# Regrouping the attention of a decoder block between dense products: four groups of small products become three

## The chip, the cores and the metric

The kernel runs on one core of a Trainium2 chip. The metric is the device time of one execution in microseconds (us), the median of several runs. The engines are called TensorE (PE in the profile; its weight loads are PEld), VectorE (DVE), ScalarE (ACT), GpSimd (POOL) and SyncE (SP, which here only issues transfers).

## The reference

One decoder layer over 256 tokens of 1024 channels, in float32. Two attention branches of 8 heads with 64 channels each run side by side; their outputs are gated and summed, and a gated feed-forward block with a short convolution follows.

```
h = rms_norm(x, attn_norm_g)
qa, ka, va, qb, kb, vb, f_logit, g_logit = split(h @ w_in)
qa, ka = partial_rope(rms_norm(heads(qa))), partial_rope(rms_norm(heads(ka)))
o_a = moba_attention(qa, ka, va)          # one block of 256 keys: causal softmax
qb, kb = rms_norm(heads(qb)), rms_norm(heads(kb))
log_f = log_sigmoid(f_logit + b_forget)
o_b = forgetting_attention(qb, kb, vb, log_f)   # scores + c[t] - c[s], c = cumsum(log_f)
gates = sigmoid(g_logit + b_gate)
merged = gates[0] * (o_a @ w_branch_moba) + gates[1] * (o_b @ w_branch_fox)
x = x + merged @ w_out
u, g = split(rms_norm(x, ffn_norm_g) @ w_ffn_up)
x = x + (silu(causal_conv(g)) * u) @ w_ffn_down
```

With 256 tokens the first branch's block selection leaves each query its own block, so both branches are causal attention over all 256 keys; the second adds a bias from the running sum c.

## The kernel before

**Dense products.** Every weight is split into a high half and a low half of fewer bits (`load`, lines 116 to 139): ScalarE copies the raw weight into `whi` (L134), VectorE subtracts to get `wlo` (L135). The activations are split in the same way, and a dense product is three products, high by high, high by low and low by high, summed in one PSUM bank. `project` (L236) does this for q, k and v of both branches (`project(0..5)`) and, through `gate` (L443), for eight half products of the gates. One half of a weight feeds 12 products of 512 columns on TensorE (L245).

**Loads.** `use` (L141) asks for a half of a weight and first calls `load` up to five halves ahead. Where `state["hold"]` is true it doesn't, and a later explicit `load(...)` catches up. While `state["behind"]` names two instructions, the split on ScalarE is ordered behind the first and that on VectorE behind the second.

**PSUM.** All products go to eight banks of 512 columns, taken in turn (`bank`, `banks`); a new use waits until the engines that read the old content are done.

**Attention.** It runs as small products put between the dense ones:

- `turn_one` (L282) turns a finished q or k with 16 transposes (L289) into two banks; two copies with a gain bring it to SBUF, on ScalarE (L297) or, where named in `vector`, on VectorE (L295).
- `forget_c` (L352) sums log_f by a product (L357), copies on VectorE (L359, L360), stores to DRAM and loads it back spread over all partitions, both issued from ScalarE's queue (L362, L363). `forget_bias` (L365) adds the mask on VectorE.
- `scores(branch, pair)` (L377) does two heads: products on TensorE into two banks (L387), four masked reductions that read the banks on VectorE (L392), four exponentials on ScalarE (L395), and a reciprocal and four scalings on VectorE (L397, L400).
- `turn(branch, pair)` (L406) turns the probabilities of two heads with 12 transposes (L414) into two banks and copies them out, two copies on ScalarE (L404) or, where named, on VectorE (L416).
- `values(branch, pairs)` (L420) multiplies two pairs' turned probabilities with v (L428) into one bank; ScalarE takes the high half (L430), VectorE the low (L431).

**Order.** TensorE runs in the order in which the code is written (`manual_schedule` names it alone). On the other engines a planner orders the instructions when the program is built, by its own estimate of when each becomes ready: of those that are ready on an engine, it takes the one written first. That order is then fixed. The stretch that matters is lines 482 to 530. There the attention's small products form four groups between dense products: in the middle of the second k's product (L487 to L495), after the first gate half product (L503 to L505), after the fourth (L512 to L517), and after the eighth (L523 to L530).

Of the kernel before, what the change touches and what calls it, by code (L numbers as in the profile page):

```python
# [30 lines left out]
RB, HB, AHEAD = 3, 6, 5  # L31
# [10 lines left out]
def decoder_block(ctx, tc, a, out):  # L42
    nc = tc.nc
# [6 lines left out]
    def T(shape, tag, bufs=1, dt=F32):  # L50
        return sb.tile(shape, dt, tag=tag, bufs=bufs, name=tag)
# [33 lines left out]
    pos = {c: i for i, c in enumerate(chunks)}  # L85
    split = {}
    state = {"next": 0, "raw": None, "ahead": AHEAD, "hold": False, "behind": None}
# [18 lines left out]
    def home(n):  # L106

        slot = (n - state["base"] - AHEAD - 1) % (HB + 3) if AHEAD < state["ahead"] else 3
        if slot > 2:
            return T([P, 1024], "whi", HB, F32R), T([P, 1024], "wlo", HB, F32R)  # L110
        if slot == 2:
            return [T([P, 1024], "qn", 3, F32R) for _ in range(2)]
        both = T([P, 2, 1024], ("V", "bias")[slot], 1, F32R)
        return both[:, 0], both[:, 1]

    def load(upto):
        while state["next"] <= min(upto, 2 * len(chunks) - 1):
            i, h = divmod(state["next"], 2)
            state["next"] += 1
            if i < 2:  # L120
                lead(2 * i + h)
                continue
            c = chunks[i]
            if h == 0:
                w = 1024 if i == 2 else 2048
                src = a[c[0]]
                for j in (c[1] - (c[0] == "qkv"), *c[2:]):
                    src = src[j]
                raw = state["raw"] = T([P, 2048], "raw", RB)
                for j in range(2048 // w):  # L130
                    nc.sync.dma_start(raw[:, j * w:(j + 1) * w], src[:, j * w:(j + 1) * w])
            raw = state["raw"][:, h * 1024:(h + 1) * 1024]
            hi, lo = home(2 * i + h)
            whi = nc.scalar.activation(hi, raw, AF.Copy)  # L134
            wlo = nc.vector.tensor_tensor(lo, raw, hi.bitcast(F32), op=ALU.subtract)  # L135
            if state["behind"]:
                after(whi, state["behind"][0])
                after(wlo, state["behind"][1])
            split[c, h] = (hi, lo, whi)
# [142 lines left out]
    def turn_one(n, br, isk, vector=()):  # L282
        dst = T([P, 4, S], f"{'qk'[isk]}T{br}")
        two = banks()
        for t in range(NT):
            for b in range(4):
                c = slice((4 * t + b) * HD, (4 * t + b + 1) * HD)
                for r, (rows, eye) in enumerate(parts):
                    nc.tensor.transpose(two[r][:, c], n[rows, t, 2 * b:2 * b + 2].rearrange("p h d -> p (h d)"), eye)  # L289
        for r in range(2):  # L290
            to = dst.rearrange("p b (t r c) -> p r t b c", t=NT, r=2)[:, r]
            src = two[r].rearrange("p (t b c) -> p t b c", t=NT, b=4)
            gain = col(C_QG + 2 * br + isk)
            if r in vector:
                last = nc.vector.tensor_scalar_mul(to, src, gain)  # L295
            else:
                first = nc.scalar.activation(to, src, AF.Copy, scale=gain)  # L297
                last = first
        turned[br, isk] = dst
        return first, last  # L300
# [51 lines left out]
    def forget_c():  # L352
        lf = fg["lf"]
        cp = bank()
        c0, c1 = (cp[:NH, t * P:(t + 1) * P] for t in range(NT))
        for t, c in enumerate((c0, c1)):
            nc.tensor.matmul(c, lf[:, t], tri, start=True, stop=True)  # L357
        cT = T([P, 2, 384], "pT", 4)[:NH, 0, 0:S]
        nc.vector.tensor_copy(cT, cp[:NH, 0:S])  # L359
        nc.vector.tensor_scalar_add(cT[:, P:S], cT[:, P:S], cT[:, P - 1:P])  # L360
        cd = dr.tile([NH, S], F32, name="cd")
        nc.scalar.dma_start(cd, cT)  # L362
        nc.scalar.dma_start(bias[:, :, P:P + S], bass.AP(tensor=cd.tensor, offset=cd.offset, ap=[[0, P], [S, NH], [1, S]]))  # L363
# [13 lines left out]
    def scores(br, pair):  # L377
        s = T([P, 2, 384], "s", 4)
        nm = T([P, 2, 2], "nm", 4)
        l = T([P, 2, 2], "l", 4)  # L380
        sps = banks()
        for t in range(NT):
            for j in range(2):
                dst = sps[j][:, t * P:t * P + (t + 1) * P]
                ts, us = slice(t * P, (t + 1) * P), slice(0, (t + 1) * P)
                rows = parts[j][0]
                nc.tensor.matmul(dst, turned[br, 0][rows, pair, ts], turned[br, 1][rows, pair, us], start=True, stop=True)  # L387
        for j in range(2):
            h = 2 * pair + j
            sp = sps[j]  # L390
            for i, c in enumerate((slice(0, 128), slice(128, 384))):
                nc.vector.tensor_tensor_reduce(s[:, j, c], sp[:, c], mask3[:, c] if br == 0 else bias[:, h, c],  # L392
                                               scale=1.0, scalar=3e38, op0=ALU.add, op1=ALU.min, accum_out=nm[:, j, i:i + 1])
            for i, c in enumerate((slice(0, 128), slice(128, 384))):
                last_exp[:] = [nc.scalar.activation(s[:, j, c], s[:, j, c], AF.Exp, scale=-1.0, bias=nm[:, j, i:i + 1], accum_out=l[:, j, i:i + 1])]  # L395
        r = T([P, 2, 2], "r", 4)
        nc.vector.reciprocal(r, l)  # L397
        for j in range(2):
            for i, c in enumerate((slice(0, 128), slice(128, 384))):
                last_norm[:] = [nc.vector.tensor_scalar_mul(s[:, j, c], s[:, j, c], r[:, j, i:i + 1])]  # L400
        probs[br, pair] = s
# [4 lines left out]
    def turn(br, pair, copy=copy):  # L406
        s = probs.pop((br, pair))
        pT = T([P, 2, 384], "pT", 4)
        two = banks()
        for j in range(2):  # L410
            for b in range(3):
                c = slice((3 * j + b) * HD, (3 * j + b + 1) * HD)
                for r, (rows, eye) in enumerate(parts):
                    nc.tensor.transpose(two[r][:, c], s[rows, j, b * P:(b + 1) * P], eye)  # L414
        for r in range(2):
            done = copy(pT.rearrange("p j (b r c) -> p r j b c", b=3, r=2)[:, r], two[r][:, 0:384].rearrange("p (j b c) -> p j b c", j=2, b=3))  # L416
        probs[br, pair] = pT
        return done

    def values(br, two):  # L420
        op = bank()
        for n, pair in enumerate(two):
            pT = probs.pop((br, pair))
            for i, c in enumerate((slice(0, 256), slice(256, 384))):
                for j in range(2):
                    o = HD * j
                    vc = br * W4 + (2 * pair + j) * HD
                    nc.tensor.matmul(op[o:o + HD, n * S + i * P:(n + 1) * S], V[:, i, vc:vc + HD], pT[:, j, c], start=(i == 0), stop=(i == 1))  # L428
        oh, ol = (o[:, 4 * br + two[0]:4 * br + two[0] + 2].rearrange("p b t -> p (b t)") for o in heads)
        high = nc.scalar.activation(oh, op, AF.Copy)  # L430
        nc.vector.tensor_tensor(ol, op, oh.bitcast(F32), op=ALU.subtract)  # L431
        return high
# [10 lines left out]
    def gate(c):  # L443
        g, h = divmod(c, 2)
        if h == 0:
            state["gate"] = banks()
        project(("wg", c), state["gate"], h)
        if h == 1:
            for t in range(NT):
                nc.vector.scalar_tensor_tensor(gates[t][g], state["gate"][t], rs[:, t:t + 1], bg[g], op0=ALU.mult, op1=ALU.add)  # L450
# [19 lines left out]
    k0 = finish_qk(pk, 0, 1)  # L470
# [10 lines left out]
    q1 = finish_qk(pq, 1, 0)  # L481
# [3 lines left out]
    state["hold"] = True  # L485
    project(4, pk, 1, (0,))
    turn_one(q0, 0, 0, (1,))  # L487
    state["behind"] = turn_one(k0, 0, 1, (1,))
    state["hold"] = False
    load(2 * pos["qkv", 4, 1] + AHEAD)  # L490
    state["behind"] = None
    forget_c()
    turn_one(q1, 1, 0)
    for pair in range(3):
        scores(0, pair)  # L495
    project(4, pk, 1, (1,))
    k1 = finish_qk(pk, 1, 1)
# [2 lines left out]
    project(5, pv, 1)  # L500
    finish_v(pv, 1)
    gate(0)
    state["behind"] = turn(0, 0), turn(0, 1, nc.vector.tensor_copy)  # L503
    scores(0, 3)
    turn_one(k1, 1, 1)  # L505
    forget_bias()
    load(2 * pos["wg", 1] + AHEAD)
    state["behind"] = None
    gate(1)
    gate(2)  # L510
    gate(3)
    turn(0, 2)  # L512
    turn(0, 3)
    for pair in range(4):
        scores(1, pair)
    values(0, (0, 1))
    values(0, (2, 3))  # L517
    gate_bias()
    for c in (4, 5, 6):
        gate(c)  # L520
# [314 lines left out]
```

## Time and profile before

| | us |
|---|---|
| median of three runs | 352.56 (352.04 to 352.76) |
| the profiled execution | 352.11 |
| its span in the trace | 350.2 |
| TensorE busy | 345.7 |
| VectorE busy | 284.9 |
| ScalarE busy | 218.9 |
| dense products of `project`, share of the chain (L245) | 30% |
| scores, turnings and values, share of the chain (L387, L414, L428) | 1%, 1%, 2% |

The profile comes from one execution. The chain that ended last is followed back from the last instruction, at each step to what released it. A timeline lists start, length, engine, line and operation; TensorE's matmuls are pipelined, so that lengths overlap and the distance between starts tells what each costs. An idle time in square brackets is followed by what ended it.

### The profile page before, as it was taken

Reading aid. Unit: us, or ns where it says so; the run is one execution under the profiler, and the core shown is the slowest. Engines: PE = TensorE matmul, PEld = TensorE weight load, DVE = VectorE, ACT = ScalarE, POOL = GpSimd, SP = SyncE. Lnnn points to the kernel's source line nnn. Section 1 sums busy time; section 2 is a strip of 40 time slices with the busy share of each in tenths; the row PEclk is TensorE's granted clock in tenths of the full one; section 3 lists DMA queues with packets and bytes.
Section 4 is the critical chain, followed back from the end, with each engine's and each line's share of the span. In section 5 each row is a group of like instructions: output and inputs, shape, how many; then the busy total and the mean of one; then the engine's idle time right before and its main releaser. Section 6 shows DMA issues by size and latency. Waiting matters only on the chain.

```text
span 350.2 us, 5351 instructions
## 1 busy us (share of the span) xinstructions
PE 345.7 (99%) x2021; PEld 301.9 (86%) x2021; DVE 284.9 (81%) x530; ACT 218.9 (63%) x386; POOL 2.7 (1%) x11
## 2 busy tenths in 40 slices
PE   9999999999999999999999999999999999999995
PEld 4888887888888888888899989989898999989885
DVE  5999997998697678896489999897869888798733
ACT  4968564966489465644496966675665765666420
POOL 0000000000000000000010000000000000000000
PEclk9999999999999999999999999999999999999999
DMA  7998873765570617567119566674564655560003
GB/s 272 402 347 287 320 295 121 241 247 218 168 268 3 233 30 250 211 263 281 58 60 371 192 234 240 223 260 138 223 240 134 242 225 177 199 226 3 0 0 122
DMA packets 14250, 70.23 MB, mean 201 GB/s; under 512 B 1640, under 2 KB 4848, under 8 KB 6800
## 3 DMA queue, kind: packets, MB, share of 16 engines
q1 hardware_dynamic: 12944, 68.69, 54.5%
q10 hardware_dynamic: 1200, 1.06, 0.9%
q8 instruction: 16, 0.26, 0.3%
q0 software_dynamic: 80, 0.13, 0.2%
q14 instruction: 10, 0.08, 0.1%
HBM read 68.82 MB, written 1.06 MB: 200 GB/s over the span
## 4 chain that ended last, share of the span: by engine, by line
PE 98%; ACT 1%; issue 0%; DVE 0%
PE bank L245 30%; PE bank L670 22%; PE bank L717 16%; PE bank L671 11%; PE bank L551 6%; PE bank L599 6%; PE bank L428 2%; PE bank L387 1%; PE bank L169 1%; PE bank L414 1%; ACT qT L297 1%; PE bank L612 0%; PE bank L564 0%; PE bank L289 0%; PE bank L319 0%
## 5 line engine op out<-in xcount | busy, mean ns | idle before, releaser
L135 DVE TENSOR_TENSOR wlo<-raw,whi 128x1024 fp32r<-128x1024 f32 x94 | 114.1, 1222 | 19.9 <-ACT whi L134 19.5
L134 ACT ACTIVATE whi<-raw 128x1024 fp32r<-128x1024 f32 x94 | 97.7, 1053 | 35.3 <-PE bank L245 12.3
L670 PE MATMUL bank<-pp,whi 128*128 128x512 f32 x232 | 76.7, 383 | 0.0
L671 PE MATMUL bank<-pp,wlo 128*128 128x256 f32 x232 | 63.2, 273 | 0.0
L670 PEld LDWEIGHTS bank<-pp,whi 128*128 128x128 f32 x232 | 43.9, 189 | 6.1
L245 PE MATMUL bank<-whi,xh 128*128 128x512 f32 x160 | 48.4, 384 | 0.1
L245 PE MATMUL bank<-wlo,xh 128*128 128x512 f32 x160 | 47.8, 380 | 0.0
L245 PE MATMUL bank<-whi,xl 128*128 128x512 f32 x160 | 47.6, 379 | 0.0
L671 PEld LDWEIGHTS bank<-pp,wlo 128*128 128x128 f32 x232 | 44.5, 192 | 0.2
L245 PEld LDWEIGHTS bank<-whi,xh 128*128 128x128 f32 x160 | 29.6, 189 | 6.1 <-ACT whi L102 1.3
L245 PEld LDWEIGHTS bank<-wlo,xh 128*128 128x128 f32 x160 | 30.0, 189 | 4.8 <-DVE wlo L103 0.5
L245 PEld LDWEIGHTS bank<-whi,xl 128*128 128x128 f32 x160 | 30.2, 189 | 4.4 <-DVE xl L163 0.2
L717 PE MATMUL bank<-whi,qT 128*128 128x512 f32 (+1 forms) x92 | 27.8, 370 | 0.0
L686 DVE TENSOR_TENSOR sq<-bank,lows 128x256 f32<-128x256 f32 x44 | 18.1, 418 | 4.3 <-ACT lows L685 4.3
L691 ACT ACTIVATE s<-sq,sm 128x256 f32<-128x256 f32 x22 | 13.1, 596 | 12.3 <-DVE sq L687 12.3
L685 ACT ACTIVATE lows<-bank 128x256 f32<-128x256 f32 x44 | 15.8, 371 | 7.4 <-PE bank L671 7.4
L717 PEld LDWEIGHTS bank<-whi,qT 128*128 128x128 f32 x92 | 17.2, 189 | 2.3
L670 PE MATMUL bank<-pp,bias 128*128 128x512 f32 x56 | 18.7, 382 | 0.0
L717 PE MATMUL bank<-wlo,qT 128*128 128x512 f32 (+1 forms) x46 | 17.0, 370 | 0.0
L551 PE MATMUL bank<-whi,pp 128*128 128x512 f32 x64 | 17.0, 382 | 0.0
L694 ACT ACTIVATE s<-s 128x256 f32<-128x256 f32 x22 | 9.1, 415 | 11.2 <-DVE s L693 11.2
L687 DVE TENSOR_TENSOR sq<-sq,rsB 128x512 f32<-128x512 f32 x22 | 15.2, 690 | 0.6
(171 smaller groups left out, 568.8 us busy)
## 6 DMA issues: line engine op xcount, KB each, us to landing
raw<-in_wu SPq DMA_DIRECT2D x22, 1024.0 KB, 4.8
raw<-in_wd SPq DMA_DIRECT2D x11, 1024.0 KB, 4.8
raw<-in_qkv SPq DMA_DIRECT2D x9, 1024.0 KB, 5.6
raw<-in_wg SPq DMA_DIRECT2D x8, 1024.0 KB, 4.8
raw<-in_wb SPq DMA_DIRECT2D x4, 1024.0 KB, 6.0
raw<-in_wo SPq DMA_DIRECT2D x4, 1024.0 KB, 4.9
lead<-in_lead SPq DMA_DIRECT2D x8, 384.0 KB, 6.3
raw<-in_qkv SPq DMA_DIRECT2D x2, 512.0 KB, 7.8
```

The costliest lines, as they stand in the source:

```text
L134: whi = nc.scalar.activation(hi, raw, AF.Copy)
L135: wlo = nc.vector.tensor_tensor(lo, raw, hi.bitcast(F32), op=ALU.subtract)
L245: nc.tensor.matmul(pt[t], lhs[:, k, t * P:(t + 1) * P], rhs, start=(k == 0 and i == 0), stop=(k == KT - 1 and i == 2))
L551: nc.tensor.matmul(ps_[t], lhs[:, t * P:(t + 1) * P], rhs, start=(k == 0 and i == 0), stop=(k == 3 and i == 2))
L599: nc.tensor.matmul(acc[t][dh], lhs[:, k, t * P:(t + 1) * P], rhs, start=(k == 0 and i == 0), stop=(k == KT - 1 and i == 2))
L670: nc.tensor.matmul(two[i], wh[:, w], both, start=(k == 0), stop=False)
L671: nc.tensor.matmul(two[i][:, 0:S], wl[:, w], high, start=False, stop=(k == KT - 1))
L685: nc.scalar.activation(lows[:, i:i + 1].rearrange("p b (a t) -> p b a t", a=2), apart(two[i][:, S:2 * S], 1), AF.Copy)
L686: nc.vector.tensor_tensor(halves(ev[:, i:i + 1]), apart(two[i][:, 0:S], 1), halves(lows[:, i:i + 1]), op=ALU.add)
L687: nc.vector.tensor_tensor(ev, ev, rs2[:, None, :].to_broadcast([P, 2, S]), op=ALU.mult)
L691: nc.scalar.activation(cv, g, AF.Identity, scale=col(C_CW + 2 * NF + f), bias=col(C_CB + f))
L717: nc.tensor.matmul(o, lhs, rhs, start=(first and i == 0), stop=(end and i == 2))
```

## The change

Only the order in which the attention's parts are written changes; no operation is added or left out, save that one copy of the second branch's turned q, and one of its k, go to VectorE in place of ScalarE.

- In the first group the decay products (`forget_c`) move ahead of the second q's turning, one of that q's two copies goes to VectorE, the held weight split is ordered behind those copies in place of the first k's, and all four pairs of first-branch scores follow in place of three.
- The second group, after the first gate half product, goes. The bias step stays there. Its weight split is called for by the gate product itself.
- The third group moves from behind the fourth gate half product to behind the third, that is into the middle of the second gate. Into it go the second k's turning (one copy on VectorE), all four turnings of first-branch probabilities, the values of the first branch, and the four pairs of second-branch scores, mixed. Weight splits are held over the third gate half product and ordered behind the last turning's copies.
- The last group stays.

```diff
     turn_one(q0, 0, 0, (1,))
-    state["behind"] = turn_one(k0, 0, 1, (1,))
+    turn_one(k0, 0, 1, (1,))
+    forget_c()
+    state["behind"] = turn_one(q1, 1, 0, (1,))
     state["hold"] = False
     load(2 * pos["qkv", 4, 1] + AHEAD)
     state["behind"] = None
-    forget_c()
-    turn_one(q1, 1, 0)
-    for pair in range(3):
+    for pair in range(4):
         scores(0, pair)
     project(4, pk, 1, (1,))
     k1 = finish_qk(pk, 1, 1)
...
     gate(0)
-    state["behind"] = turn(0, 0), turn(0, 1, nc.vector.tensor_copy)
-    scores(0, 3)
-    turn_one(k1, 1, 1)
     forget_bias()
-    load(2 * pos["wg", 1] + AHEAD)
+    gate(1)
+    state["hold"] = True
+    gate(2)
+    turn_one(k1, 1, 1, (1,))
+    turn(0, 0)
+    turn(0, 1, nc.vector.tensor_copy)
+    scores(1, 0)
+    turn(0, 2)
+    scores(1, 1)
+    values(0, (0, 1))
+    state["behind"] = 2 * (turn(0, 3),)
+    state["hold"] = False
+    load(2 * pos["wg", 2] + 1 + AHEAD)
     state["behind"] = None
-    gate(1)
-    gate(2)
+    scores(1, 2)
+    values(0, (2, 3))
+    scores(1, 3)
     gate(3)
-    turn(0, 2)
-    turn(0, 3)
-    for pair in range(4):
-        scores(1, pair)
-    values(0, (0, 1))
-    values(0, (2, 3))
     gate_bias()
```

## The prediction, made before the changed kernel was run

> **What bounds the kernel now.** I read the page first, for the span and for the chain that ended last.
>
> ```profile
> span 350.2 us, 5351 instructions
> ...
> PE 98%; ACT 1%; issue 0%; DVE 0%
> ```
>
> TensorE is the chain: 98% of the span. So the change is worth what it adds to or takes from TensorE's own time, plus any new wait of TensorE, and a wait in the middle arrives at the end in full. Next I read the busy time by stretches, for the stretch that the change rearranges (columns: stretch, length, then PE, weight loads, VectorE, ScalarE, GpSimd, then clock, DMA share, GB/s).
>
> ```profile
> 80.00:104.00 24.00, 24.00 (x203) 20.41 (x200) 20.29 (x54) 16.30 (x40) 0.00 (x0) 1.00 0.65 225
> ```
>
> TensorE has no idle time here and the granted clock is 1.00. VectorE (20.29 of 24.00) and ScalarE (16.30) are busy, but nobody waits for them: that is the cover the change may use up. Then the timeline of TensorE (start, length, line, operation), around the second attention group:
>
> ```profile
> 79.04 0.59 PE L245 MATMUL bank<-whi,xl 128*128 128x512 f32 x2
> 79.56 0.97 PE L414 MATMUL bank<-cst,s 64*128 64x64 f32 x24
> 80.37 0.88 PE L387 MATMUL bank<-kT,qT 64*128 64x128 f32 x8
> 81.08 0.74 PE L289 MATMUL bank<-cst,qn 64*128 64x64 f32 x16
> 81.75 0.70 PE L245 MATMUL bank<-whi,xh 128*128 128x512 f32 x2
> 82.28 0.59 PE L245 MATMUL bank<-wlo,xh 128*128 128x512 f32 x2
> 82.72 0.59 PE L245 MATMUL bank<-whi,xl 128*128 128x512 f32 x2
> ```
>
> Take the start-to-start steps, not the lengths, since the lengths overlap. A pair of wide products steps 0.44 us (82.28 to 82.72). Entering the group costs 79.56 - 79.04 - 0.44 = 0.08 more, and the first pair after it 0.53 instead of 0.44, 0.09 more: a group costs 0.17 us beside its work. Two turnings of probabilities take 0.81 (0.40 each), one pair of heads' scores 0.71, and the whole group 2.19 (79.56 to 81.75). The third group:
>
> ```profile
> 97.49 0.97 PE L414 MATMUL bank<-cst,s 64*128 64x64 f32 x24
> 98.29 2.85 PE L387 MATMUL bank<-kT,qT 64*128 64x128 f32 x32
> 101.07 2.82 PE L428 MATMUL bank<-pT,V 128*64 128x256 f32 x32
> 103.82 0.70 PE L245 MATMUL bank<-whi,xh 128*128 128x512 f32 x2
> ```
>
> Four pairs of scores in 2.78 (0.70 a pair), values in 2.75 (0.69 a pair), the group in 6.33, with no wait in it: all turnings stand ahead of all scores, so their copies on ScalarE come before the exponentials, and the values come last. The first group:
>
> ```profile
> 56.22 1.22 PE L289 MATMUL bank<-cst,qn 64*128 64x64 f32 x32
> 57.37 0.60 PE L357 MATMUL bank<-cst,lf 128*8 128x128 f32 x4
> 57.90 0.71 PE L289 MATMUL bank<-cst,qn 64*128 64x64 f32 x16
> 58.55 2.75 PE L387 MATMUL bank<-kT,qT 64*128 64x128 f32 x24
> 61.23 0.70 PE L245 MATMUL bank<-whi,xh 128*128 128x512 f32 x2
> ```
>
> Here three pairs of scores take 2.68, where 3 x 0.70 = 2.10 would do: TensorE waits about 0.58 inside. The group lasts 5.01; one turning of q or k takes 1.15 / 2 = 0.58. ScalarE in the same place:
>
> ```profile
> 56.96 0.69 ACT L297 ACTIVATE qT<-bank,sm 128x512 f32<-128x512 f32 x1 [4.76 <-PE bank L289]
> 57.55 0.68 ACT L297 ACTIVATE kT<-bank,sm 128x512 f32<-128x512 f32 x1
> 58.12 1.05 ACT L134 ACTIVATE whi<-raw 128x1024 fp32r<-128x1024 f32 x1
> 59.07 0.69 ACT L297 ACTIVATE qT<-bank,sm 128x512 f32<-128x512 f32 x1
> 59.07 0.52 ACTq L362 DMA_DIRECT2D cd<-pT  x1
> 59.64 0.69 ACT L297 ACTIVATE qT<-bank,sm 128x512 f32<-128x512 f32 x1
> 60.68 0.40 ACT L395 ACTIVATE s<-s,nm 128x128 f32<-128x128 f32 x1 [0.35 <-DVE nm L392]
> ```
>
> The second q's two copies (59.07 and 59.64) stand behind a weight split (58.12) and end at 60.33; the third pair's scores need the two banks that they empty. That is the 0.58. A ScalarE copy of this form steps 0.57, and starts about 0.17 after its turning (56.22 + 0.58 = 56.80 to 56.96); I use 0.2 for a hand-over between engines.
>
> **The first group, changed.** It removes the 0.58: the second q's copies now go one to ScalarE (ready 58.55 + 0.2 = 58.75, ends 59.32) and one to VectorE, and the split goes behind them. VectorE's rows:
>
> ```profile
> 57.67 0.74 DVE L295 TENSOR_SCALAR kT<-bank,sm 128x512 f32<-128x512 f32 x1
> 58.32 0.40 DVE L359 COPY pT<-bank 8x256 f32<-8x256 f32 x1
> 58.76 0.27 DVE L360 TENSOR_SCALAR pT<-pT 8x128 f32<-8x128 f32 x1
> 59.21 1.23 DVE L135 TENSOR_TENSOR wlo<-raw,whi 128x1024 fp32r<-128x1024 f32 x1 [0.17 <-ACT whi L134]
> 60.35 0.28 DVE L392 CUSTOM_DVE_ANT_0 s<-bank,cst 128x128 f32<-128x128 f32 x1
> ...
> 61.46 0.29 DVE L392 CUSTOM_DVE_ANT_0 s<-bank,cst 128x128 f32<-128x128 f32 x1
> ```
>
> VectorE's copy of this form steps 0.65 (57.67 to 58.32), so the new one runs 59.03 to 59.68, before the third pair's scores at 58.55 + 1.40 = 59.95. It adds a fourth pair, 0.70, and with that a new wait. Of eight banks two hold the second k's running product, and the other six go round: the fourth pair gets the banks of the first, and must wait until VectorE has reduced that pair (1.11 a pair, 60.35 to 61.46). If VectorE reduces at once: 59.68 + 1.11 + 0.2 = 60.99, and TensorE's second product of the fourth pair comes at about 60.8: 0.2 lost. But the low half of the weight split, written ahead of the scores, is ready 1.09 after its high half starts (58.12 to 59.21), that is 59.32 + 1.09 = 60.41, just when VectorE passes from one head to the next; it steps 1.14 (59.21 to 60.35), and if it slips in there the wait is 1.3. If it goes ahead of both heads, 60.41 + 1.14 + 1.11 + 0.2 = 62.86, and the wait is 2.1. In this trace it went first (59.21, after waiting 0.17 for it), but it was ready sooner. I take 0.75, halfway between 0.2 and 1.3, as the rows leave a tie; 2.1 stays for the range, and the lower end is 0.2, since the order of reductions and bank cannot be had sooner. The group: 1.15 + 0.53 + 0.65 + 2.80 + 0.75 = 5.88, against 5.01: **+0.87**. The decay products moved past the second q's turning take their store and broadcast with them on ScalarE's queue; the store waits for VectorE's 58.76 row as now and may put the q copy back by 0.3, still ahead of 59.95. The broadcast has time:
>
> ```profile
> bias<-cd ACTq DMA_DIRECT2D x1, 1024.0 KB, 8.5
> ```
>
> 8.5 us from about 61.2 ends before 70, and its first reader, the bias step, is written after the first gate product, beyond 74. The fourth pair puts about 1.75 on ScalarE and 1.11 of reductions on VectorE ahead of the second k's finishing; that k is now turned two gate products (about 10 us) later than before, which covers it.
>
> **The old second group goes.** Its work reappears elsewhere; as a group it gives back 2.19 + 0.17 = **-2.36**. The weight split that was ordered behind its copies now follows the second gate product's use, without such an order.
>
> **The new second group.** TensorE's work: the second k's turning 0.58, four turnings 1.60, four pairs of scores 2.80, values 2.75: 7.73, against 6.33 for the third group now. The rest is waits. The rows for ScalarE's and VectorE's share, from their timelines:
>
> ```profile
> 81.89 0.40 ACT L395 ACTIVATE s<-s,nm 128x128 f32<-128x128 f32 x1
> ...
> 83.64 1.25 ACT L297 ACTIVATE kT<-bank,sm 128x512 f32<-128x512 f32 x2
> ```
>
> ```profile
> 98.56 1.61 ACT L404 ACTIVATE pT<-bank 128x384 f32<-128x384 f32 x4
> ```
>
> ```profile
> 126.12 1.95 DVE L416 COPY pT<-bank 128x384 f32<-128x384 f32 x4
> ```
>
> The first of these is the row on which the forecast hangs. The second k's turning ended on TensorE at 81.75, and ScalarE did not copy it until 83.64: it first ran the four exponentials of the pair written ahead of it (1.75, 81.89 to 83.64). So a copy waits for exponentials that were written earlier and are ready. Nobody cared there. In the new order the copies of turnings 2 and 3 are written behind the exponentials of second-branch pairs 0 and 1, and the values need them at once.
>
> Counting from the group's first transpose: k turned 0.58; copied by ScalarE 0.78 to 1.37, by VectorE 0.78 to 1.43. Turning 0 ends 0.98, its ScalarE copies (0.40 each) run 1.37 to 2.17. Turning 1 ends 1.38, its VectorE copies (0.49 each) 1.58 to 2.54. Scores 0 wait for k: 1.63 to 2.33. Turning 2 waits for two banks: 2.37 to 2.77. Scores 1: 2.77 to 3.47. VectorE reduces pair 0 from 2.54; the first exponential follows 0.33 later (60.35 to 60.68), so ScalarE has them 2.87 to 4.62. Values of pairs 0 and 1: 3.47 to 4.85. ScalarE copies turning 2: 4.62 to 5.42. Turning 3 needs one of those banks: 5.22 to 5.62. Scores 2 need the other: 5.62 to 6.32. Values of pair 2: to 7.01. ScalarE meanwhile: exponentials of pair 1, 5.42 to 7.17; the high half of the first values (same width as a q copy, 0.57), 7.74; turning 3, 8.54. Values of pair 3 start at 8.74, **1.73 late**, end 9.43; scores 3 end 10.13. The waits are 0.25, 0.04, 0.37 and 1.73. The group takes 10.13 against 6.33: **+3.80**. Bounds: no wait at all, 7.73, +1.40; every step as above is also near the upper end, for ScalarE is then busy without a gap from 2.87.
>
> Held splits: two halves (the fifth gate product's second and the sixth's first), behind turning 3's copies. TensorE reaches the first of them only after the fourth product and half of the fifth, 18 pairs of 0.44 or 7.9 us after the group; a split steps 0.95 on ScalarE (58.12 to 59.07) and 1.14 on VectorE, so both are hidden. Their loads are not ordered behind anything on ScalarE: on SyncE's queue they wait for a free buffer only. Without that cover each would cost about 1.1.
>
> **The sum.** +0.87 - 2.36 + 3.80 = **+2.3 us**. The profiled execution took 352.11 (its span 350.2 and 1.9 around it), which gives 354.4; the median of the three runs is 352.56, 0.45 above it, which gives **354.8**. With every wait free it would be (0.12 - 2.36 + 1.40) = -0.84, 351.7; with the worst split order +3.65, 356.2.
>
> **Rivals.** (1) *ScalarE copies turning 3 before the exponentials of pair 1.* The order on ScalarE is the planner's, and if it reckons VectorE slower than it is, the copies are ready first. They then run from 5.82 to 6.62, values of pair 3 follow at 7.01 without a wait, the group takes 8.40, and the change comes to 0.3 to 1.4 - 2.36 + 2.07 = 0.0 to +1.1, by the middle 353.1: no change. It decides where exponentials of pair 1 are ready after 5.8, though pair 1 has been reduced by 2.54 + 2 x 1.11 = 4.76. Against it speaks the 83.64 row. Chance 0.18. (2) *All waits are hidden*, copies of turning 2 going ahead too and the first group's split going last: up to -0.84, taken as 351.8, the only way to faster, and by little. It needs k's copy, two banks and both copies in time; chance 0.06. (3) *The clock drops over the new gaps.* The rows above show 1.00 with no gap, so they cannot say. If the twelve pairs of the next gate product ran at half speed, that costs up to 12 x 0.44 = 5.3 on top, 360.1. Chance 0.03. The Trainium skill, "TensorE: Matmul & The Clock Gate", section "A second HAM failure mode: psum-queue depth-cycling", holds that short idles between matmul groups while banks cycle can throttle the clock; its section "HAM oscillation — how this bites in real kernels" asks for gaps over about 3.4 us, more than any gap forecast here. By the first the time would be rival 3's, by the second the sum stands; no run yet shows which.
>
> **How the numbers follow.** The forecast's mechanism has 0.73, rivals 0.18, 0.06 and 0.03. A measurement of this kernel can tell about 0.2%, 0.7 us, from no change. Slower by more: 0.73 less a little for smaller waits, plus the clock: 0.75. Within: rival 1 and that little, 0.19. Faster: rival 2, 0.06. The range runs from 352.4, which takes in nearly all of rival 1, to 356.0, which leaves out most of the split-first order and the clock: some 0.15 to 0.2 lies outside. The likeliest case alone spans 354.0 to 356.0.
>
> **What would show it.** In the changed kernel: a weight load of the values (L428) idle for 1 to 2 us in the second group, released by ScalarE's copies at L404; on ScalarE, four exponentials (L395) between the copies of turnings 2 and 3; the second group near 10 us and the first near 5.9, with its fourth pair released by VectorE's reductions (L392); steps of 0.44 between wide products elsewhere. Wrong, if the values follow scores 2 without a gap, if the second group takes under 9 us, or if the time moves while both groups sum to the old 13.5 us.

## The result, and the profile after

| | before | after | forecast |
|---|---|---|---|
| median, us | 352.08 (6 runs) | 354.35 (6 runs) | 354.8, against 352.56 shown then |
| ratio | 1 | 1.0059, 95% interval 1.0049 to 1.0069 | 1.006 |
| span of the profiled execution, us | 350.2 | 352.0 | |

The kernel became slower by 0.6%. The profiled execution is the fastest of the changed kernel's six (353.9), so the traces differ by less than the medians. The page of the changed kernel has other engines on its chain now:

```profile
span 352.0 us, 5349 instructions
...
PE 96%; ACT 2%; DMA 1%; DVE 0%; issue 0%
```

Most of ScalarE's 2% is one stretch of the second group, 93.17 to 98.77, in which the chain runs through exponentials and copies; that is the path to TensorE's waits, not their length: TensorE itself stands 0.34 and 0.85 in it. DMA's 1% is a load at the start of the program, which the change does not touch. TensorE's timeline in the first group (start, length, line, operation):

```profile
56.05 1.22 PE L289 MATMUL bank<-cst,qn 64*128 64x64 f32 x32
57.20 0.60 PE L357 MATMUL bank<-cst,lf 128*8 128x128 f32 x4
57.73 0.71 PE L289 MATMUL bank<-cst,qn 64*128 64x64 f32 x16
58.39 3.22 PE L387 MATMUL bank<-kT,qT 64*128 64x128 f32 x32
61.54 0.70 PE L245 MATMUL bank<-whi,xh 128*128 128x512 f32 x2
```

The group takes 61.54 - 56.05 = 5.49 us (5.01 before, 5.88 forecast). Its four pairs of scores take 3.15 where 2.80 would do, 0.35 more. Not all of that is waiting: in the run with eleven groups below, a pair of scores that ends a group takes 0.86 (96.57 to 97.43) in place of 0.70, and no wait shows there, so about 0.2 is left for the fourth pair's wait. The new second group:

```profile
90.23 0.71 PE L289 MATMUL bank<-cst,qn 64*128 64x64 f32 x16
90.78 0.92 PE L414 MATMUL bank<-cst,s 64*128 64x64 f32 x24
91.91 0.93 PE L387 MATMUL bank<-kT,qT 64*128 64x128 f32 x8 [0.21 <-DVE kT L295]
92.64 0.56 PE L414 MATMUL bank<-cst,s 64*128 64x64 f32 x12
93.01 0.90 PE L387 MATMUL bank<-kT,qT 64*128 64x128 f32 x8
93.84 1.52 PE L428 MATMUL bank<-pT,V 128*64 128x256 f32 x16
95.30 0.74 PE L414 MATMUL bank<-cst,s 64*128 64x64 f32 x12
95.82 0.93 PE L387 MATMUL bank<-kT,qT 64*128 64x128 f32 x8
97.09 0.87 PE L428 MATMUL bank<-pT,V 128*64 128x256 f32 x8 [0.34 <-DVE nm L392]
98.81 0.87 PE L428 MATMUL bank<-pT,V 128*64 128x256 f32 x8 [0.85 <-ACT pT L404]
99.61 0.93 PE L387 MATMUL bank<-kT,qT 64*128 64x128 f32 x8
100.47 0.70 PE L245 MATMUL bank<-whi,xh 128*128 128x512 f32 x2
```

10.24 us, where the third group took 6.33 and the forecast was 10.13. The values come in two pieces with a gap before each: pair 2's at 97.09, released by VectorE's reductions, and pair 3's at 98.81, released by ScalarE's copies, 8.58 us after the group's start (8.74 forecast). ScalarE's timeline at that place:

```profile
94.94 0.84 ACT L404 ACTIVATE pT<-bank 128x384 f32<-128x384 f32 x2
95.68 0.40 ACT L395 ACTIVATE s<-s,nm 128x128 f32<-128x128 f32 x1
...
96.55 0.58 ACT L430 ACTIVATE pp<-bank 128x512 fp32r<-128x512 f32 x1
97.03 0.40 ACT L395 ACTIVATE s<-s,nm 128x128 f32<-128x128 f32 x1
...
97.91 0.85 ACT L404 ACTIVATE pT<-bank 128x384 f32<-128x384 f32 x2
```

Between the copies of turning 2 (94.94) and of turning 3 (97.91) stand the four exponentials of second-branch pair 1 (two of them under the dots) and the high half of the first values. Turning 3 had ended on TensorE when scores 2 began, at 95.82: its copies stood 2 us in the queue. VectorE, for the other gap:

```profile
95.06 0.18 DVE L397 RECIPROCAL r<-l 128x4 f32<-128x4 f32 x1 [0.82 <-ACT s L395]
...
95.48 1.00 DVE L400 TENSOR_SCALAR s<-s,r 128x128 f32<-128x128 f32 x4
96.40 0.28 DVE L392 CUSTOM_DVE_ANT_0 s<-bank,bias 128x128 f32<-128x128 f32 x1
...
96.61 0.42 DVE L392 CUSTOM_DVE_ANT_0 s<-bank,bias 128x256 f32<-128x256 f32 x1
```

The reductions of pair 1's second head (96.40 and 96.61) follow pair 0's reciprocal and scalings, for which VectorE sat idle 0.82; the bank that they free at 97.03 is the one that the values of pair 2 take at 97.09. The same rows show that the exponentials of that second head could not start before about 96.7, when turning 3 was long done: its copies stood behind two exponentials that were not even ready, since the order on ScalarE is fixed when the program is built. ScalarE lost no time by it, because the high half of the first values (96.55) filled the place. The sum by the traces: first group +0.48, old second group -2.36, new one 10.24 - 6.33 = +3.91, together +2.03; the attention began 0.17 earlier (56.05 against 56.22), which leaves 1.86, and the spans differ by 1.8. The medians differ by 2.27; the changed kernel's median lies 0.45 above its profiled execution.

### The profile page after: what moved, and what is told of

It is laid out like the page before. It is cut to its first block, busy times and chain, and to the rows that moved or that the text cites. A ratio compares the mean times of both kernels' runs of the same rounds, so it can differ in the third digit from the quotient of the medians.

```text
span 352.0 us, 5349 instructions
## 1 busy us (share of the span) xinstructions
PE 346.0 (98%) x2021; PEld 302.2 (86%) x2021; DVE 285.4 (81%) x532; ACT 217.2 (62%) x384; POOL 2.7 (1%) x11
## 4 chain that ended last, share of the span: by engine, by line
PE 96%; ACT 2%; DMA 1%; DVE 0%; issue 0%
PE bank L245 30%; PE bank L674 22%; PE bank L721 16%; PE bank L675 11%; PE bank L555 6%; PE bank L603 6%; PE bank L387 1%; PE bank L428 1%; ACT s L395 1%; DMA lead<-in_lead 1%; PE bank L289 1%; PE bank L616 0%; PE bank L414 0%; ACT pT L404 0%; PE bank L568 0%; PE bank L319 0%
```

## The experiments

The theory: a copy out of PSUM runs behind what was written ahead of it on its engine, and TensorE stands until it is made. The rivals: ScalarE as a whole has too much to do; or three groups are too dense for the banks, whatever the order. All ratios are to the kernel before, with a 95% interval. Each `diff` is against the changed kernel unless the text says otherwise, and `...` in it stands for lines left out.

**The last turning's copies on VectorE.**

```diff
-    state["behind"] = 2 * (turn(0, 3),)
+    state["behind"] = 2 * (turn(0, 3, nc.vector.tensor_copy),)
```

> The changed kernel with one edit: the last turning of first-branch probabilities is copied out by VectorE in place of ScalarE. Theory (a copy waits behind the work of scores written ahead of it, whichever engine makes it): VectorE has the second pair's reductions, the first pair's scalings and the low half of the first values ahead of it, so the copies end at about the same point as on ScalarE, 0 to 0.3 us later; the time stays at the changed kernel's, 0.5 to 0.8% above the kernel before. Rival (ScalarE alone has too much to do in this group, VectorE has room): the copies end 1 us earlier, and the time is 0.3 to 0.4% above the kernel before.

Measured: 354.18 us, 1.0058 (1.0046 to 1.0071), as the changed kernel. TensorE's values of pair 3 start 8.68 us after the group (90.82 to 99.50), and VectorE's rows show why:

```profile
96.07 1.00 DVE L400 TENSOR_SCALAR s<-s,r 128x128 f32<-128x128 f32 x4
...
97.76 0.69 DVE L431 TENSOR_TENSOR pp<-bank,pp 128x512 fp32r<-128x512 f32 x1
98.37 0.55 DVE L416 COPY pT<-bank 128x384 f32<-128x384 f32 x1
98.83 0.17 DVE L397 RECIPROCAL r<-l 128x4 f32<-128x4 f32 x1
98.92 0.53 DVE L416 COPY pT<-bank 128x384 f32<-128x384 f32 x1
```

The copies end at the same point of the group as on ScalarE (8.63 and 8.53 after its start). Ahead of them stand pair 0's scalings, pair 1's last reductions (under the dots) and the values' low half. It is not ScalarE's load alone: either engine has work of the scores and values in front of them.

**Exponentials of pair 1 behind the copies.** `scores` is cut in two, products and reductions first, the rest by a second call; each exponential of pair 1 is ordered behind the copy.

```diff
-    scores(1, 1)
+    rest = scores(1, 1, True)
     values(0, (0, 1))
     state["behind"] = 2 * (turn(0, 3),)
+    rest(state["behind"][0])
```

> The changed kernel with the four exponentials of second-branch pair 1 ordered behind the copies of turning 3 on ScalarE; nothing else changes. Theory (those exponentials stand ahead of the copies that TensorE waits for): the copies end about 1.6 us earlier; the values of pair 2 still wait for a bank as before, so the second group shrinks from 10.24 to about 9.2 us and the time is about 0.3% above the kernel before in place of 0.6%. Rival (ScalarE's total work bounds the group, or another wait comes right behind): less than 0.3 us is won, and the time stays 0.5% or more above.

Measured: 353.05 us, 1.0028 (1.0019 to 1.0036). TensorE, then ScalarE (in this kernel L437 is the values, L399 the exponentials, L413 the copies, L439 the values' high half):

```profile
97.26 1.52 PE L437 MATMUL bank<-pT,V 128*64 128x256 f32 x16 [0.33 <-DVE nm L392]
98.71 0.93 PE L387 MATMUL bank<-kT,qT 64*128 64x128 f32 x8
99.57 0.70 PE L245 MATMUL bank<-whi,xh 128*128 128x512 f32 x2
```

```profile
95.85 0.58 ACT L439 ACTIVATE pp<-bank 128x512 fp32r<-128x512 f32 x1
96.33 0.87 ACT L413 ACTIVATE pT<-bank 128x384 f32<-128x384 f32 x2
97.07 0.41 ACT L399 ACTIVATE s<-s,nm 128x128 f32<-128x128 f32 x1
```

The copies go first, both values come in one piece, and the group, begun at 90.40, takes 9.17. All of ScalarE's work is still there. The gap ahead of pair 2 is left.

**Pair 0 too.** Pair 0's exponentials behind the copies of turning 2, its scalings written behind pair 1's reductions.

```diff
-    scores(1, 0)
-    turn(0, 2)
-    scores(1, 1)
+    rest0 = scores(1, 0, True)
+    copied = turn(0, 2)
+    rest1 = scores(1, 1, True)
+    rest0(copied)
...
+    rest1(state["behind"][0])
```

> As the run before, and the exponentials of second-branch pair 0 also ordered behind the copies of turning 2, with their reciprocal and scalings written behind the reductions of pair 1. Theory: the bank that the values of pair 2 wait for comes free about 1.7 us earlier, the copies of turning 2 come earlier too; the second group takes about 8.5 us in place of 10.24, and the time is 0.1 to 0.2% above the kernel before. Rival (the bank wait has nothing to do with the order of scalings and reductions on VectorE): no better than the run before, 0.3%.

Measured: 352.40 us, 1.0011 (1.0002 to 1.0020); the group takes 8.60 (90.24 to 98.84), and the values start without a gap at 96.53:

```profile
96.53 1.52 PE L437 MATMUL bank<-pT,V 128*64 128x256 f32 x16
97.98 0.93 PE L387 MATMUL bank<-kT,qT 64*128 64x128 f32 x8
98.84 0.70 PE L245 MATMUL bank<-whi,xh 128*128 128x512 f32 x2
```

With the one edit and this one, 1.64 of the 2.5 us that the group took beyond its bare 7.73 are gone, by order alone.

**The first group alone**, in the kernel before (the `diff` is against it).

```diff
-    state["behind"] = turn_one(k0, 0, 1, (1,))
+    turn_one(k0, 0, 1, (1,))
+    forget_c()
+    state["behind"] = turn_one(q1, 1, 0, (1,))
...
-    forget_c()
-    turn_one(q1, 1, 0)
-    for pair in range(3):
+    for pair in range(4):
...
-    scores(0, 3)
     turn_one(k1, 1, 1)
```

> The kernel before with the change's first group alone: decay products ahead of the second q, one of its copies on VectorE, four pairs of scores; the second group keeps its place and loses the fourth pair. Theory (the first group costs 0.48 us more and saves the 0.71 us of the pair in the second): 0.2 us faster than the kernel before, 0 to 0.1% by the ratio, hardly to be told from none. Rival (the extra pair delays VectorE so that the second k, or the split weights, come late): slower by 0.5 us or more, 0.15% or more above.

Measured: 351.54 us, 0.9987 (0.9978 to 0.9996): a little faster than before, by 0.3 in the traces' groups (first group 5.49 for 5.01, second 1.41 for 2.19). No wait of TensorE for the second k or for the weights of the stretch shows. The change's loss lies in the new second group.

**Unmixed.** All turnings, then all scores, then all values; the held splits now follow the values.

```diff
     turn(0, 1, nc.vector.tensor_copy)
-    scores(1, 0)
     turn(0, 2)
-    scores(1, 1)
+    turn(0, 3)
+    for pair in range(4):
+        scores(1, pair)
     values(0, (0, 1))
-    state["behind"] = 2 * (turn(0, 3),)
+    state["behind"] = 2 * (values(0, (2, 3)),)
...
-    scores(1, 2)
-    values(0, (2, 3))
-    scores(1, 3)
```

> The changed kernel with its second group unmixed: second k and all four turnings first, then the four pairs of scores, then all values, the held splits behind the values. Theory (the cost is that copies are written behind exponentials): all copies now come before any exponential; what is left are waits for k's turning (0.25), two bank pairs (0.3) and the reductions (0.2), the group takes about 8.5 us, the time is 0 to 0.15% above the kernel before. Rival (three groups hold too much work for ScalarE and VectorE in one place, whatever the order): 9.5 us or more, 0.4% or more above.

Measured: 352.23 us, 1.0004 (0.9995 to 1.0013), the group 8.37 (90.81 to 99.18). The same three groups without the mixing cost nothing that can be told from the kernel before: the mixing was the loss, not the density.

**Values early, copies shared.** `None` gives a turning's first copy to ScalarE and its second to VectorE.

```diff
...
+    turn(0, 0, None)
+    turn(0, 1, None)
+    turn(0, 2, None)
     turn_one(k1, 1, 1, (1,))
...
+    turn(0, 3, None)
+    values(0, (0, 1))
     scores(1, 0)
...
     scores(1, 1)
...
+    scores(1, 2)
+    state["behind"] = 2 * (values(0, (2, 3)),)
...
     scores(1, 3)
```

> The changed kernel with its second group in another order and with each turning's two copies shared by ScalarE and VectorE: turnings 0, 1, 2, the second k, turning 3, values of pairs 0 and 1, scores 0 to 2, values of pairs 2 and 3, scores 3. Theory: every copy is made one step or more before TensorE needs it and before any exponential; the group takes 7.7 to 8.0 us, its bare work, and the time is 0.1 to 0.15% below the kernel before. Rival (a group of this size always waits for banks or copies): 8.5 us or more, no faster than the kernel before.

Measured: 352.18 us, 1.0007 (0.9998 to 1.0015), the group 8.39 (90.71 to 99.10): a miss, as 7.7 to 8.0 were expected. VectorE took the values' low half first, sat idle for it, and the reductions started late:

```profile
95.20 0.69 DVE L431 TENSOR_TENSOR pp<-bank,pp 128x512 fp32r<-128x512 f32 x1 [1.23 <-ACT pp L430]
95.81 0.28 DVE L392 CUSTOM_DVE_ANT_0 s<-bank,bias 128x128 f32<-128x128 f32 x1
```

The copies were in time. The three pairs of scores that follow take 2.35 in place of 2.10, and the trace names a reduction as what the weights of the values behind them waited for; that the late reductions cost the rest was not tried by itself.

**Eleven groups.** The first group as above; each turning, k, pair of scores and pair of values by itself, between and in the middle of gate products; `between(c, step)` puts a step in the middle of gate product c.

```diff
...
+    turn(0, 0)
...
+    between(1, lambda: turn(0, 1, nc.vector.tensor_copy))
+    turn_one(k1, 1, 1)
+    between(2, lambda: turn(0, 2))
+    turn(0, 3)
+    between(3, lambda: scores(1, 0))
...
```

> The first group as in the change, and the work of the second and third groups of the kernel before taken apart into eleven groups of one step each, between and in the middle of six gate products: nine groups more than in the run with the first group alone. Theory (a group costs 0.17 us at its two edges, as the timeline's steps show): 1.5 us slower than that run, 0.25 to 0.35% above the kernel before. Rival (the edges are hidden or only an effect of how ends are modelled): same as that run, 0.1% below the kernel before.

Measured: 354.77 us, 1.0075 (1.0062 to 1.0087). Against the first group alone that is 0.88% or 3.1 us for nine groups, 0.34 us each: the theory that a group has a price holds, but only half of it had been counted. One of the groups:

```profile
79.39 0.59 PE L245 MATMUL bank<-whi,xl 128*128 128x512 f32 x2
79.92 0.59 PE L414 MATMUL bank<-cst,s 64*128 64x64 f32 x12
80.44 0.70 PE L245 MATMUL bank<-whi,xh 128*128 128x512 f32 x2
80.98 0.59 PE L245 MATMUL bank<-wlo,xh 128*128 128x512 f32 x2
```

The entry costs 0.10 (79.92 - 79.39 - 0.43), the turning steps 0.52 in place of 0.40, and the first pair after it 0.54 in place of 0.43: 0.33. The 0.12 in the last operation of a group I had not counted, as it hides in that operation's step; it differs with the operation (0.16 for a pair of scores, 96.57 to 97.43). The Trainium skill, "TensorEngine Tiling (Array Packing)", section "Key Properties", says that a change of tiling mode drains TensorE; the small products here use half the array's rows or columns, and the 0.33 agrees with it without proving that cause. A pointer to it: two small products of 128x128, which use the whole array, stand between wide pairs at 45.54 in the kernel before (L328), and start 0.43 after the pair ahead of them (45.11), without an entry cost.

**No hold.**

```diff
     gate(1)
-    state["hold"] = True
     gate(2)
...
-    state["behind"] = 2 * (turn(0, 3),)
-    state["hold"] = False
-    load(2 * pos["wg", 2] + 1 + AHEAD)
-    state["behind"] = None
+    turn(0, 3)
```

> The changed kernel without the hold in the second gate: its weight splits are asked for by the third gate product itself and not ordered behind the last turning. Theory (the hold keeps split halves off VectorE while TensorE waits for banks): one low half stands between the second k's copy and turning 1's on VectorE and delays the scores of pair 1 by about 1 us; 0.8 to 0.95% above the kernel before. Rival (the hold does nothing, as its price was put at nothing): 0.6%, as the changed kernel.

Measured: 355.06 us, 1.0080 (1.0066 to 1.0094), the group 11.14 (90.25 to 101.39). VectorE:

```profile
91.71 1.21 DVE L135 TENSOR_TENSOR wlo<-raw,whi 128x1024 fp32r<-128x1024 f32 x1
92.84 1.01 DVE L416 COPY pT<-bank 128x384 f32<-128x384 f32 x2
```

One low half stands between k's copy and turning 1's, and the group is 0.9 longer. The hold as a whole is worth that here; the planner's order on ScalarE changed with it (a high half stands ahead of k's copy), so the 0.9 is not the price of this one row.

**The split between the reductions that the fourth pair waits for.** Four groups: the run with the first group alone, which the `diff` is against, with the second q's copies both on ScalarE and the decay products behind.

```diff
     turn_one(k0, 0, 1, (1,))
-    forget_c()
-    state["behind"] = turn_one(q1, 1, 0, (1,))
+    state["behind"] = turn_one(q1, 1, 0)
+    forget_c()
```

> The kernel of the run with the first group alone (four groups), with the second q's copies both on ScalarE and the decay products behind that q's turning. In this order the planner puts the low half of the held weight split between the reductions of the second head of first-branch pair 0. Theory (the fourth pair's banks come free by those reductions, so a split of 1.14 us in between holds TensorE up): the first group takes 6.3 to 6.5 us in place of 5.49, 0.1% above the kernel before. Rival (banks are not what the fourth pair waits for): 5.2 to 5.5 us, 0.1 to 0.2% below the kernel before.

Measured: 353.08 us, 1.0023 (1.0014 to 1.0031), the first group 6.62 (57.11 to 63.73), a little beyond the 6.3 to 6.5 expected. TensorE within the four pairs of scores, then VectorE with the split between the two reductions of the first pair's second head:

```profile
62.89 0.92 PE L387 MATMUL bank<-kT,qT 64*128 64x128 f32 x6 [1.01 <-DVE nm L392]
```

```profile
61.26 1.23 DVE L135 TENSOR_TENSOR wlo<-raw,whi 128x1024 fp32r<-128x1024 f32 x1
62.40 0.42 DVE L392 CUSTOM_DVE_ANT_0 s<-bank,cst 128x256 f32<-128x256 f32 x1
```

**The split behind them**, against the run before.

```diff
-    state["hold"] = False
-    load(2 * pos["qkv", 4, 1] + AHEAD)
-    state["behind"] = None
     for pair in range(4):
         scores(0, pair)
+    state["hold"] = False
+    load(2 * pos["qkv", 4, 1] + AHEAD)
+    state["behind"] = None
```

> As the run before, with the held split asked for after the four pairs of scores, so that it stands behind pair 0's reductions. Theory: no wait of the fourth pair is left, the first group takes 5.1 to 5.25 us, the time is 0.2% below the kernel before. Rival (as above): no difference from the run before.

Measured: 351.74 us, 0.9982 (0.9973 to 0.9990), the first group 5.37 (56.34 to 61.71), a little over the expected 5.25. The two runs differ in one split's place and by 1.25 us in the group: the fourth pair's banks wait for those reductions. This kernel and the one with the first group alone are the only two whose interval lies below 1, and by less than 0.2%.

**Three groups, as good as I could order them.** That first group, and the order of the values-early run with values 2 and 3 ahead of scores 2.

> Three groups: the first group of the run before, and the second group in the order turnings 0, 1, 2, second k, turning 3, values of pairs 0 and 1, scores 0 and 1, values of pairs 2 and 3, scores 2 and 3, each turning's copies shared by both engines. Theory: the second group takes 8.0 to 8.2 us, nearly its bare work; with the group saved the time is 0.1 to 0.2% below the kernel before, no clear gain over four groups. Rival (fewer groups win by themselves, once the waits are gone): 0.3% or more below.

Measured: 352.11 us, 0.9991 (0.9982 to 1.0000), the group 8.21 (90.60 to 98.81). Three groups, with most waits gone, are about level with the kernel before. Against the run above, four groups with the same first group (0.9982), they are rather 0.3 us behind, though the intervals overlap: they save a group's edges, 0.33, and give back more in waits that the separate groups had hidden under dense products.

## Why the prediction was right

The direction, the place and the size were right, and the runs show the cause. That +2.3 forecast meets +2.27 between the medians so closely is partly luck: in the traces the three terms come to +2.03, the first 0.39 below the forecast and the last 0.11 above it, the spans differ by 1.8, and the 0.45 by which the changed kernel's median lies above its profiled execution happens to fill the gap.

- **The second group** (+3.80 forecast, +3.91 measured). Its largest term, the wait of pair 3's values for turning 3's copies behind pair 1's exponentials, had the right end (8.74 forecast, 8.58 measured), and ordering those exponentials behind the copies took 1.07 us off the group. The step that failed in detail is "Values of pair 2: to 7.01": they started 6.86 after the group did (97.09) in place of 6.32, and ended at 7.55, since VectorE had pair 0's scalings ahead of pair 1's last reductions, an order that the forecast had not followed. That wait lay under the longer one, so the sum did not see it; the third experiment did. The forecast also had pair 1 reduced by 4.76, and it was at 6.80. Turning 3's copies still ended at 8.53 (8.54 forecast), because the values' high half ran in the middle of the exponentials and not behind them, which left ScalarE without a gap; that part of the match is luck.
- **The first group** (+0.87 forecast, +0.48 measured). The 0.75 taken for the fourth pair's wait was too much: 0.35 with the end of the group, about 0.2 without it. The 0.58 read as waiting in the group before holds the same 0.15 of the group's end. The tie came out for the low end, as VectorE's low half at 60.56 stood behind both heads' reductions. The other end, the split between the heads, is real: 1.01 us of TensorE idle in the run that has it.
- **The old second group** (-2.36). The trace agrees; its edges are counted in full, as 0.17 outside and the rest in the last step of its 2.19. Only taken as the price of a group the 0.17 is wrong: it is 0.33.
- **The hold at nothing** was right as to the held splits themselves; that the hold saves 0.9 us I had not said.
- **The rivals.** That ScalarE copies turning 3 first did not happen, although its condition came true: the second head's exponentials were ready only after 5.8, about 6.5 after the group's start, and still went first. Forced by order it gave 1.0028 of the kernel before, where the 353.1 worked out was 1.0015 of 352.56; the bank wait ahead of pair 2 is most of the difference (group 9.17 against 8.40, pair 2's values at 6.86 against 6.32). That all waits hide did not happen in any run of three groups. The clock stayed at full speed over the gaps (columns as in the prediction):

```profile
90.00:101.00 11.00, 9.60 (x132) 6.94 (x131) 8.73 (x36) 9.28 (x29) 0.00 (x0) 1.00 0.01 2
```

Granted clock 1.00 with TensorE busy 9.60 of 11.00 and gaps up to 0.85. Of the two sections of the Trainium skill's "TensorE: Matmul & The Clock Gate", the trace agrees with "HAM oscillation — how this bites in real kernels", which asks for gaps over about 3.4 us. "A second HAM failure mode: psum-queue depth-cycling" speaks of frequent short idles and gives no number; the three idles of this group (0.21, 0.34 and 0.85) did not bring it about.

## What to carry to other kernels

Where one engine is busy all the time and the others are covered, count for each small step on it the copy that must come back before the next, and what is written ahead of that copy on its engine: here copies of 0.8 us in all stood 2 us behind four exponentials and another copy, whether or not these were ready. When groups are merged, the dense work that hid these returns goes away; keep turnings ahead of scores and reductions ahead of scalings. Weigh the 0.33 us saved per group against the waits laid bare. What can be moved without such a return, as the fourth pair of scores here, is the part worth keeping.

## What the runs showed of the hardware that I had not expected

A group of small products costs TensorE 0.33 to 0.34 us beside its work, not the 0.17 seen at its outer edges: for a turning, 0.10 to enter, 0.12 in its last operation and 0.11 in the first wide pair behind it (nine more groups, 3.1 us). The granted clock did not fall for an idle gap of 0.85 us in a group with nine switches between kinds of products.
